# One transformer block in split fp32 on one core: w_out as a Strassen product, its weights and the first gate_up weights split during the projections, sums and low halves on GpSimd

## The chip, the cores and the metric

The kernel runs on one core of a Trainium2 chip. The metric is device microseconds for one execution of the whole block. A core has five engines, each with its own instruction queue that runs in order: TensorE (PE in the profile, its weight loads PEld) for matmuls, VectorE (DVE), ScalarE (ACT) and GpSimd (POOL) for elementwise work, and SyncE (SP), which issues most DMA transfers; GpSimd issues some as well. They wait for each other on semaphores.

## The reference, cut to what matters

```python
D_MODEL = SEQ = 1024; ATTN_WIDTH = CONV_WIDTH_CH = 512; FFN_HIDDEN = 2816; DEPTH = 1

def mixer(h, w_in, b_f, conv_w, w_branch, w_out):
    proj = jnp.einsum("bsd,dn->bsn", h, w_in)
    q, k, v, f_logit, g_b, g_c, hc, gate_conv, gate_attn = jnp.split(proj, _SPLITS, axis=-1)
    ya = g_b * causal_depthwise_conv(g_c * hc, conv_w)
    ...
    yb = forgetting_attention(q.reshape(shp), k.reshape(shp), v.reshape(shp), logf)
    ya_d = jnp.einsum("bsc,cd->bsd", ya, w_branch[0])
    yb_d = jnp.einsum("bsc,cd->bsd", yb, w_branch[1])
    merged = jax.nn.sigmoid(gate_conv) * ya_d + jax.nn.sigmoid(gate_attn) * yb_d
    return jnp.einsum("bsd,de->bse", merged, w_out)

def swiglu(h, w_gate_up, w_down):
    gu = jnp.einsum("bsd,df->bsf", h, w_gate_up)
    g, u = jnp.split(gu, 2, axis=-1)
    return jnp.einsum("bsf,fd->bsd", jax.nn.silu(g) * u, w_down)

    # reference, per layer
    h = rmsnorm(x, norm_mix_pre[l])
    m = mixer(h, w_in[l], b_f[l], conv_w[l], w_branch[l], w_out[l])
    x = x + rmsnorm(m, norm_mix_post[l])
    h = rmsnorm(x, norm_ffn_pre[l])
    f = swiglu(h, w_gate_up[l], w_down[l])
    x = x + rmsnorm(f, norm_ffn_post[l])
```

All tensors are float32, with 1024 rows of 1024.

## The kernel before

**Split products.** Each float32 operand is kept as two float32r tiles, a high half (ScalarE copies and rounds) and a low half (VectorE subtracts the high half from the original). `split` makes both; `mm3` issues three matmuls per 128x128 weight block: high by high, low by high, high by low.

**Strassen.** In the projections, gate_up and down, a product is done on 2x2 blocks with seven block products in the Winograd form: A11, A12, A22 of the left operand, its sums S1 to S4, and B11, B21, B22 and the sums T1 to T4 of the right operand. A block product (`prod`) is 4 blocks x 3 = 12 matmuls of 128x512, and a job of seven is 84. `strassen` issues them in the order S2, S1, S3, S4, A22 in two PSUM banks, b2 and b3: VectorE must have taken b2 into a sum before S3 adds to it, and b3 before S4 does. The product A11 (`first`, b1) is copied out by ScalarE before A12 adds to the same bank.

**Stages, in order.** The projections: 18 jobs, to about 400 us. Attention with the branch products `pba`, to 567 us. The second branch product `pbb`: 16 tiles (2 column halves `n` x 8 blocks `d` of 128), each with a load of the saved gate `sg` and then, on VectorE, gate times product and an addition into `um`, the merged rows, held transposed (feature blocks by 1024 rows). During its first half `w_out` is loaded in 8 pieces and split into `woh` and `wol`. Then w_out itself: `e_mm(st)` splits 128 rows of `um` and multiplies by all of w_out, 2 halves x 8 blocks x 3 matmuls (`pm`); `e_norm(st)` norms, adds x, norms again, and 8 transposes (`tp`) put the rows back into `um`. Then the f stage: `f_first(f)` for seven of the gate_up jobs loads the job's first weights from `w_gate_up`, splits them, and makes A11 and A12, which go to `pre_dram` until the job needs them; `h2_sums(sl)` makes T1 to T4 and B22 of the right operand of gate_up between them. Then gate_up (771 to 1126 us) and down (to 1343 us).

**Order.** Every call goes through `InOrder.call` at line 76, so that nearly all rows of the profile have that line; they are told apart by the names of their tiles. The Tile framework orders each engine's instructions by its own estimates; calls within a `strict` stretch keep the order of the code on the engines named. Tiles are reused in rings (`raw`, `hi`, `lo`, `sx`): a load or a write waits until the last reader of the tile's former contents is done.

## Time and profile before

| | |
|---|---|
| median of three runs | 1350.23 us (1350.2 to 1351.78) |
| the profiled execution's own time | 1350.04 us |
| its span in the profile | 1348.2 us |
| PE busy | 1328.5 us, 6753 matmuls |
| DVE, ACT, POOL busy | 932.3, 535.2, 127.2 us |
| granted PE clock | 0.999 |

Busy times are sums over the span; each engine's idle time matters only where PE waits for that engine. In the views a row names engine, operation, output tile, input tiles and shape; "<-" behind a bracketed time names what ended the idle time. The share of DMA is of the core's 16 DMA engines.

### The profile page before, as it was taken

Reading aid. Unit: us, or ns where it says so; the run is one execution under the profiler, and the core shown is the slowest. Engines: PE = TensorE matmul, PEld = TensorE weight load, DVE = VectorE, ACT = ScalarE, POOL = GpSimd, SP = SyncE. Lnnn points to the kernel's source line nnn. Section 1 sums busy time; section 2 is a strip of 40 time slices with the busy share of each in tenths; the row PEclk is TensorE's granted clock in tenths of the full one; section 3 lists DMA queues with packets and bytes.
Section 4 is the critical chain, followed back from the end, with each engine's and each line's share of the span. In section 5 each row is a group of like instructions: output and inputs, shape, how many; then the busy total and the mean of one; then the engine's idle time right before and its main releaser. Section 6 shows DMA issues by size and latency. Waiting matters only on the chain.

```text
span 1348.2 us, 17709 instructions
## 1 busy us (share of the span) xinstructions
PE 1328.5 (99%) x6753; PEld 1098.9 (82%) x6753; DVE 932.3 (69%) x1445; ACT 535.2 (40%) x851; POOL 127.2 (9%) x252
## 2 busy tenths in 40 slices
PE   9999999999999999999999999999999999999997
PEld 7978888888887778788887788888888888888886
DVE  6974668754556766775669698776677766677585
ACT  6642222243345756613547232223222323444452
POOL 0001000011112112000002121100111011000000
PEclk9999999999999999999999999999999999999999
DMA  5332422333325444362235565332323236965541
GB/s 189 118 109 86 126 70 71 105 123 109 102 82 192 158 142 165 126 218 79 94 110 175 170 200 167 102 100 80 117 102 118 93 111 240 361 235 196 161 164 63
DMA packets 153256, 186.36 MB, mean 138 GB/s; under 512 B 9409, under 2 KB 106753, under 8 KB 153170
## 3 DMA queue, kind: packets, MB, share of 16 engines
q1 hardware_dynamic: 138434, 136.67, 32.4%
q0 software_dynamic: 14736, 48.54, 9.3%
q8 instruction: 53, 0.87, 0.3%
q14 instruction: 33, 0.27, 0.1%
HBM read 136.10 MB, written 49.09 MB: 137 GB/s over the span
## 4 chain that ended last, share of the span: by engine, by line
PE 58%; DVE 3%; DMA 2%; issue 1%; ACT 1%; POOL 0%; DVEq 0%; SPq 0%; POOLq 0%; ACTq 0%
PE b L76 28%; PE pd L76 15%; PE pm L76 5%; PE pbb L76 3%; PE pba L76 2%; PE po L76 1%; PE tps L76 1%; PE sp L76 1%; DMA pre_dram<-s 1%; DMA tk<-in_w_down_dram 1%; DVE tt L76 0%; DVE lo L76 0%; PE tp L76 0%; DMA pre_dram<-c 0%; ACT tt L76 0%
## 5 line engine op out<-in xcount | busy, mean ns | idle before, releaser
L76 DVE TENSOR_TENSOR c<-c,b 128x512 f32<-128x512 f32 x195 | 132.9, 682 | 91.4 <-PE b L76 72.3
L76 DVE TENSOR_TENSOR lo<-raw,hi 128x1024 fp32r<-128x1024 f32 (+1 forms) x93 | 112.0, 1204 | 83.1 <-PE b L76 68.8
L76 ACT ACTIVATE hi<-raw 128x1024 fp32r<-128x1024 f32 (+1 forms) x100 | 101.7, 1018 | 127.9 <-PE b L76 75.7
L76 PE MATMUL b<-hth,hi 128*128 128x512 f32 x352 | 137.3, 390 | 0.0
L76 PE MATMUL b<-hth,lo 128*128 128x512 f32 x352 | 137.0, 389 | 0.0
L76 PE MATMUL b<-htl,hi 128*128 128x512 f32 x352 | 136.9, 389 | 0.0
L76 ACT ACTIVATE hi<-sx 128x1024 fp32r<-128x1024 f32 x41 | 43.5, 1062 | 220.9 <-PE b L76 195.3
L76 PEld LDWEIGHTS b<-hth,hi 128*128 128x128 f32 x352 | 66.1, 188 | 14.6 <-DVE c L76 1.0
L76 PEld LDWEIGHTS b<-hth,lo 128*128 128x128 f32 x352 | 66.1, 188 | 13.8
L76 PEld LDWEIGHTS b<-htl,hi 128*128 128x128 f32 x352 | 66.1, 188 | 13.7
L76 DVE TENSOR_TENSOR lo<-sx,hi 128x1024 fp32r<-128x1024 f32 x41 | 50.2, 1224 | 33.6 <-PE b L76 31.4
L76 PE MATMUL b<-hah,hi 128*128 128x512 f32 x176 | 69.0, 394 | 1.2 <-ACT c L76 1.2
L76 PE MATMUL b<-hal,hi 128*128 128x512 f32 x176 | 68.5, 389 | 0.0
L76 PE MATMUL b<-hah,lo 128*128 128x512 f32 x176 | 68.4, 390 | 0.0
L76 DVE TENSOR_TENSOR sx<-raw 128x512 f32<-128x512 f32 x78 | 53.6, 688 | 19.1 <-DMA raw<-in_w_in_dram 9.0
L76 PE MATMUL pd<-hi,lo 128*128 128x512 f32 x160 | 62.3, 389 | 0.0
L76 PE MATMUL pd<-hi 128*128 128x512 f32 x160 | 62.0, 390 | 0.0
L76 PE MATMUL pd<-ghi 128*128 128x512 f32 x148 | 57.6, 390 | 0.0
L76 PE MATMUL pd<-glo,ghi 128*128 128x512 f32 x148 | 57.6, 389 | 0.0
L76 PE MATMUL pd<-ghi,glo 128*128 128x512 f32 x148 | 57.6, 389 | 0.0
L76 PE MATMUL b<-hT34h,hi 128*128 128x512 f32 x136 | 53.0, 390 | 0.4 <-DVE c L76 0.4
L76 PE MATMUL b<-hT34h,lo 128*128 128x512 f32 x136 | 52.9, 389 | 0.0
(368 smaller groups left out, 3359.9 us busy)
## 6 DMA issues: line engine op xcount, KB each, us to landing
raw<-in_w_gate_up_dram SPq DMA_DIRECT2D x51, 512.0 KB, 3.8
raw<-in_w_in_dram SPq DMA_DIRECT2D x35, 512.0 KB, 3.8
a_dramS<-um POOLq DMA_DIRECT2D x44, 256.0 KB, 2.8
a_dramA<-um POOLq DMA_DIRECT2D x33, 256.0 KB, 2.8
xt<-in_x_dram SPq DMA_DIRECT2D x16, 512.0 KB, 4.3
sg<-sg_dram SPq DMA_DIRECT2D x32, 256.0 KB, 4.6
graw<-a_dramS SPq DMA_DIRECT2D x14, 512.0 KB, 4.0
sg_dram<-c POOLq DMA_DIRECT2D x24, 256.0 KB, 2.3
```

Source lines behind the costliest of these rows:

```text
L76: ins = getattr(self.engine, name)(*args, **kw)
```

## The change

**w_out as a Strassen product.** Its rows are taken in four pairs of 128-row tiles: of a pair, a11 and a12 are the two feature halves of the first tile, a21 and a22 of the second. Seven block products of 12 matmuls stand for each pair. `first(i)` and `second(i)` make A11 and A12 of all pairs ahead, `strassen` the other five products pair by pair.

**The combined weights.** B11, B21, B22 and T1 to T4 of w_out are made in the projections: `wo_load(n)`, one in each of the jobs 1 to 16, loads four 128x128 pieces, makes four differences on GpSimd, splits seven pieces (128x896) at the job's end and stores high and low halves to `wo_dram` at the start of the next. The `pbb` stage loads them back, a piece of 512 KB beside each `sg`.

**The first gate_up weights.** `pw_load(f)`, in the jobs 1 to 7, loads 512 KB, splits 128x1024 and stores two halves to `pw_dram`; `f_first` loads these instead of splitting.

**GpSimd.** It makes the sums S1 to S4 of the rows in `um` (16 of 128x512, `sums_31` and `sums_24`), the low halves of S2, S3, S1 with A22, and S4 (`gsplit`), 11 of the multiplications by the gain `gpo`, two of four subtractions of `h2_sums`, and the low half of `hc`.

```diff
@@ projections, per job
+    def wo_load(n):
+        k, c = divmod(n, 4)
+        r, h, l = w0_tiles()
+        for slot, (row, half) in enumerate(((k, 1), (k, 0), (4 + k, 0), (4 + k, 1))):
+            c0 = half * NC + c * P
+            nc.sync.dma_start(r[:, slot], wout_d[row * P : (row + 1) * P, c0 : c0 + P])
+        for o, a, b in ((4, 0, 1), (5, 3, 4), (6, 3, 0), (7, 2, 5)):
+            gtt(r[:, o], r[:, a], r[:, b], ALU.subtract)
...
     for ij, (kind, j, _, _) in enumerate(jobs):
+        for _, store in side.pop(ij - 1, ()):
+            pinned(store, "sync")
+        if 0 < ij < len(jobs) - 1:
+            side[ij] = [wo_load(ij - 1)] + ([pw_load(ij - 1)] if ij <= NPRE else [])
...
+        for ops, _ in side.get(ij, ()):
+            pinned(lambda: split(*ops), "vector", "scalar")
@@ pbb
             nc.sync.dma_start(sg, sg_dram[d][1, :, ns])
+            load_wo(*loads.pop(0))
...
-            if n == 0:
-                wr = flat(raw_t())
-                nc.sync.dma_start(wr, wout_d[d * P : (d + 1) * P, :])
-                split(woh[:, d, :], wol[:, d, :], wr)
+            if n and d == 1:
+                first_ops(0, [s4h_t(), s4h_t()], [s4l_t(), s4l_t()])
+                sx = wtile("sx", 1)
+                for i in range(2):
+                    sums_31(i, sx[:, 4 * i : 4 * i + 4])
+                sums_24(0)
@@ w_out
+    def sums_31(i, t):
+        a11, a12, a21, a22 = blocks(i)
+        s3[i] = t
+        gtt(t, a11, a21, ALU.subtract)
+        gtt(a21, a21, a22, ALU.add)
+    def sums_24(i):
+        a11, a12, s1, a22 = blocks(i)
+        gtt(a11, s1, a11, ALU.subtract)
+        gtt(a12, a12, a11, ALU.subtract)
...
+    def rest_ops(i):
+        a = slice(2 * i * P, (2 * i + 1) * P)
+        b = slice((2 * i + 1) * P, (2 * i + 2) * P)
+        hx, lx = hi_t(), lo_t()
+        gsplit(hx[:, LO], lx[:, LO], um[:, LO, a])
+        h1, l1 = hi_t(), lo_t()
+        gsplit(h1, l1, um[:, :, b])
+        gsplit(hx[:, UP], lx[:, UP], s3[i])
+        h4, l4 = s4h_t(), s4l_t()
+        gsplit(h4, l4, um[:, UP, a])
...
+    def e_norm(i, c12, c21, c22):
+        qa, qb = qas[i], st2("qb")
+        for c, acc in ((c12, qb[:, 0:1]), (c21, qa[:, 1:2]), (c22, qb[:, 1:2])):
+            square(c, acc)
+        for c, ns in ((c12, n2), (c22, n2)):
+            gtt(c, c, gpo[:, ns], ALU.mult)
+        if i < PAIRS - 1:
+            gtt(c21, c21, gpo[:, n1], ALU.mult)
...
+                nc.vector.scalar_tensor_tensor(
+                    xt[:, ns], c, rs[:, e : e + 1], xt[:, ns], op0=ALU.mult, op1=ALU.add
+                )
...
+    for step in (0, 1, 2, 3):
+        first(step)
+        if step:
+            second(step - 1)
+    second(PAIRS - 1)
...
     def f_first(f):
-        w, _ = prep_first(f_src(f)[0])
-        b1, p1 = strassen_first(w, hb, psm, fp)
+        h1, l1 = hi_t(), lo_t()
+        for t, d in zip((h1, l1), pw_dram[f]):
+            nc.sync.dma_start(f32(flat(t)), d)
+        b1 = bank(psm, "b1")
+        prod(b1, (h1[:, LO], l1[:, LO]), hb[B11], True)
...
+        copy(p1, b1)
+        prod(b1, (h1[:, UP], l1[:, UP]), hb[B21], False)
...
+    ops = rest_ops(0)
+    for i in range(PAIRS):
+        nxt = rest_ops(i + 1) if i + 1 < PAIRS else None
+        _, *cur = strassen(
+            ops, wob, psm, fe, keeps[i][:, 0], (lambda: e_turn(i - 2)) if i > 1 else None
+        )
+        e_norm(i, *cur)
+        if i > 1:
+            half_split(B11, i - 2)
+        ops = nxt
...
+    f_first(0, p1_of(0), lambda: e_turn(2))
+    h2_sums(0)
+    f_first(1, p1_of(1))
+    h2_sums(1)
+    f_first(2, p1_of(2))
+    f_first(3, p1_of(3), lambda: e_turn(3))
...
+    for sl in range(2, 4):
+        h2_sums(sl)
...
+    for f in range(4, NPRE):
+        f_first(f)
```

GpSimd's queue from the end of attention on, with the change. Ahead of it stand attention's multiplications by `mask`, as before; `um` is the merged rows, `sx` and `s4_6050` hold S3 of pairs 0, 1 and 2, `s4l` and `lo` are low halves, `raw_6081` is c21 of pair 0.

```order
L76 TENSOR_TENSOR sx_5895<-um_3800 128x512 x2
L76 TENSOR_TENSOR um_3800<-um_3800 128x4x128 x4
L76 TENSOR_TENSOR s4_6050<-um_3800 128x512
L76 TENSOR_TENSOR um_3800<-um_3800 128x4x128 x3
L76 TENSOR_TENSOR s3_6059<-um_3800 128x512
L76 TENSOR_TENSOR um_3800<-um_3800 128x4x128 x5
L76 TENSOR_TENSOR s4l_6205<-um_3800,s4h_6204 128x512
L76 TENSOR_TENSOR s4l_6219<-um_3800,s4h_6218 128x512
L76 TENSOR_TENSOR lo_6195<-um_3800,hi_6194 128x512
L76 TENSOR_TENSOR lo_6195<-sx_5895,hi_6194 128x512
L76 TENSOR_TENSOR lo_6199<-um_3800,hi_6198 128x1024
```

Before, GpSimd had DMA issues alone from here to the end. The 16 sums come first (six of them while `pbb` still runs), and the last row is the low half of S1 and A22 of pair 0.

VectorE's queue in w_out with the change, from the x updates of pair 0 on. `c12`, `raw_6081` and `c22` were multiplied by `gpo` on GpSimd; `b3_6357` is the bank of pair 1's S1, which S4 adds to next.

```order
L76 SCALAR_TENSOR_TENSOR xt_6034<-raw_6081,r1_6309,xt_6034 128x512
L76 SCALAR_TENSOR_TENSOR xt_6034<-c12_6236,r1_6309,xt_6034 128x512
L76 SCALAR_TENSOR_TENSOR xt_6036<-raw_6081,r1_6309,xt_6036 128x512
L76 SCALAR_TENSOR_TENSOR xt_6036<-c22_6250,r1_6309,xt_6036 128x512
L76 TENSOR_TENSOR c22_6384<-raw_6096,b3_6357 128x512
L76 TENSOR_TENSOR c22_6384<-c22_6384,b2_6356 128x512
```

The sums that empty the banks of one pair stand behind the x updates of the pair before; pairs 1 and 2, and 2 and 3, follow one another in the same way.

SP's queue in the projections: before, all of the weight loads of the jobs (`raw`, 512 KB each), which stood among few others.

```order
L76 DMA raw<-in_w_in_dram 128x8x128 x12
L76 DMA cb<-c_dram 128x1024 x2
L76 DMA raw<-in_w_in_dram 128x8x128 x10
L76 DMA kl<-qk_dram_67 128x1024
L76 DMA raw<-in_w_in_dram 128x8x128 x2
```

With the change, the stretch with the stores of one job's side work, the side loads of the next job and that job's first store:

```order
L76 DMA raw<-in_w_in_dram 128x8x128
L76 DMA wo_dram<-l_1808 128x7x128
L76 DMA pw_dram_128<-hg 128x1024
L76 DMA pw_dram_128<-lg 128x1024
L76 DMA r_1954<-in_w_out_dram 128x128 x4
L76 DMA rg<-in_w_gate_up_dram 128x8x128
L76 DMA raw<-in_w_in_dram 128x8x128
L76 DMA wo_dram<-h_1955 128x7x128
L76 DMA raw<-in_w_in_dram 128x8x128 x2
```

One or two loads of `raw` now stand between stores that wait for splits.

276 lines of the change are left out of this document (180 added, 96 removed).

## The prediction

> **What bounds the kernel now.** I read the page first, to see which engine is full.
>
> ```profile
> span 1348.2 us, 17709 instructions
> PE 1328.5 (99%) x6753; PEld 1098.9 (82%) x6753; DVE 932.3 (69%) x1445; ACT 535.2 (40%) x851; POOL 127.2 (9%) x252
> PEclk9999999999999999999999999999999999999999
> ```
>
> PE is busy for 99% of the span at an undisturbed clock, so time goes where matmuls go, and a stage gains only if nothing makes PE wait in their place. Next comes the chain of waits around w_out (start, length, what). `pbb` is the branch product ahead of w_out, `pm` w_out itself, `tp` the transposes after it, and the first `b` row the seven split-ahead gate_up products that I call the f stage.
>
> ```profile
> 567.59 43.52 PE pbb L76 x192
> 611.11 21.55 PE pm L76 x95
> ...
> 644.94 1.09 PE tp L76 x8
> ...
> 705.57 18.47 PE b L76 x78
> 724.06 1.22 DVE lo L76
> 725.28 1.21 DVE tt L76
> ...
> 738.43 4.49 DMA pre_dram<-s
> 745.55 4.80 DMA pre_dram<-c
> ...
> 759.69 3.78 DMA raw<-in_w_gate_up_dram
> ...
> 769.69 1.21 DVE lo L76
> 771.64 354.18 PE b L76 x1560
> ```
>
> The long PE rows give the pitch of a matmul: 354.18/1560 = 0.227 us, and 43.52/192 is the same. The chain leaves PE only between 724 and 772, in the f stage and the start of gate_up. How much PE loses there is in the busy time by stretch (columns: stretch, length, then PE, PEld, DVE, ACT and POOL busy, clock, DMA share, GB/s).
>
> ```profile
> 567.00:611.00 44.00, 44.00 (x196) 36.44 (x195) 34.02 (x46) 13.62 (x17) 0.00 (x0) 1.00 0.57 179
> 611.00:706.00 95.00, 94.65 (x444) 77.99 (x443) 59.66 (x129) 40.77 (x89) 3.77 (x7) 1.00 0.29 100
> 720.00:775.00 55.00, 51.68 (x225) 40.54 (x224) 42.38 (x62) 25.39 (x37) 9.57 (x18) 1.00 0.55 177
> ```
>
> w_out has no gap worth naming (0.35 us of 95). From 720 to 775 PE stands 55 - 51.68 = 3.3 us. That is all the idle time that the change can take away; the rest of its gain must be matmuls.
>
> **Removed: matmuls.** w_out falls from 8 row tiles x 2 halves x 8 blocks x 3 = 384 matmuls to 4 pairs x 7 products x 12 = 336. 48 x 0.227 = 10.9 us. Transposes stay 64. Against the profiled execution, 1350.04 us (1.8 above its span, and 0.2 below the median of the three runs): 1339.1.
>
> **Removed: waits in the f stage.** The first gate_up weights no longer are split there; they come in finished. Which of the 3.3 us goes? The waits of PE (total, times, longest) name the releasers, and the timeline shows one of them.
>
> ```profile
> PE b L76 <- DVE c L76: 2.5, 3, 1.5
> PE b L76 <- ACT c L76: 2.1, 3, 1.2
> ```
>
> ```profile
> 726.54 0.50 PE L76 MATMUL b<-hah,hi 128*128 128x512 f32 x1 [1.16 <-ACT c L76]
> ```
>
> The 1.16 us at 726.54 is PE waiting for ScalarE's copy of the first product out of PSUM before the second adds to it. The new f_first has the same copy in the same place, so I keep that wait and take 3.3 - 1.2 = 2.1 us as gone (bounds 0 and 3.3).
>
> **Added: GpSimd in front of every left operand.** Call the end of `pbb` 611.1. PE then does eight products whose operands VectorE and ScalarE make (8 x 12 x 0.227 = 21.8 us, until 632.9), and only then S2, S1, S3, S4, A22 of pair 0, 2.7 us each. These need GpSimd: ten sums on `um` after the last `um` addition, low halves of 512 for S4 of pairs 0 and 1 and for S2 and S3 of pair 0, and one of 1024 for S1. GpSimd's one arithmetic row and the rows of VectorE for such work are these, by form (count, busy us, mean ns, idle time before); below them, from the timeline, the rhythm of `pbb`'s end:
>
> ```profile
> L76 POOL TENSOR_TENSOR cb<-cb,mask 128x128 f32<-128x128 f32 x64 | 28.9, 460 | 103.4 <-DVE nm L76 98.4 <-DMA cb<-c_dram 4.4
> L1602 POOL MEMSET const-float32-0.0<- 128x1 f32 x1 | 0.1, 98 | 0.2 <-issue 0.2
> L76 DVE TENSOR_TENSOR um<-um 128x512 f32<-128x512 f32 x44 | 30.1, 684 | 0.3
> L76 DVE TENSOR_TENSOR lo<-um,hi 128x1024 fp32r<-128x1024 f32 x8 | 9.7, 1222 | 8.4 <-PE pm L76 8.0
> L76 DVE SCALAR_TENSOR_TENSOR um<-um,r,x2t 128x512 f32<-128x512 f32 x16 | 11.1, 747 | 0.2
> L76 DVE SCALAR_TENSOR_TENSOR tt<-xt,r,gpr 128x1024 f32<-128x1024 f32 x8 | 10.3, 1284 | 0.2
> ```
>
> ```profile
> 608.43 0.69 DVE L76 TENSOR_TENSOR sg<-sg,pbb 128x512 f32<-128x512 f32 x1 [1.31 <-PE pbb L76]
> 609.15 0.69 DVE L76 TENSOR_TENSOR um<-um,sg 128x512 f32<-128x512 f32 x1
> ```
>
> No 128x512 GpSimd operation is in this trace. Let p be its price. Lower bound: VectorE's 0.68. Upper: four of the 460 ns, 1.84. Nearest is GpSimd's own row with the fixed 98 ns of a near-empty instruction taken out: 0.098 + 4 x 0.362 = 1.55, and 3.0 for 1024. I take 1.55.
>
> The Trainium skill's "GPSIMD Engine Reference" (section 3.1) measured 4497 ns for an fp32 addition of 2048 elements per partition; a line through that and the 460 ns here would make p about 1.27, an estimate. With it the lateness worked out next would be nil and the sum 1.5 us lower; no row of 512 elements here tests it.
>
> The last `um` addition ends as the rows at 608.43 and 609.15 say, two VectorE operations after the last matmul: 612.5. Then 10 sums + 4 halves at p + one at 2p - 0.1 = 16p - 0.1 us of GpSimd. p = 1.55: 637.2. S1's low half is wanted at 632.9 + 2.7 + 0.2 = 635.8. **Late by 1.5 us.** At 1.84 it is 6.0 late, at 0.68 early.
>
> The next place is pair 1. VectorE's queue holds its x updates, which wait for GpSimd's multiplications by gpo, ahead of the sum that empties the bank for pair 2's S4; PE waits for that bank. Until the last of pair 1's multiplications GpSimd has 28 operations of p, three of 2p - 0.1 and two DMA issues of about 0.54: 34p + 0.8. PE wants the bank at 632.9 + 27.2 (two pairs) + 8.2 + 2.2 (16 transposes by the 1.09) = 670.5, less VectorE's 0.75 + 0.69: 669.0. GpSimd is there at 612.5 + 34p + 0.8: 666.0 at 1.55, in time; 675.9 at 1.84, 6.9 late (not on top of the 6.0, since a late start is already in it). So the GpSimd term is **+1.5**, bounds 0 and 7.
>
> **Moved: h2 sums and the start of gate_up.** The last transposes end at 632.9 + 54.4 + 4.4 + three f products pairs and a half (19.0) + 4.4 = 715.1. VectorE then has four subtractions and eight low halves of 512 (12 x 0.68 = 8.2, to 723.3). The raw tile that they free takes a 3.8 us load (the chain's row at 759.69), then three sums, ScalarE's 1.06, VectorE's 1.22: about 731.5. PE wants it at 715.1 + 19.0 = 734.1. Covered by 2.6 us, by the f4 to f6 products; if GpSimd's two subtractions in the chain cost 1.84 each, by 2.0. I put +0.5 for it, bounds 0 and 3 (the stall of before, moved).
>
> **Added to the projections.** Per job (84 matmuls, 19.05 us): VectorE 1.1 and, in seven jobs, 1.2 more; ScalarE the same less a little; four GpSimd operations of 0.46; five to nine DMA issues on SP, two to four of them stores that wait for splits.
>
> ```profile
> 148.00:262.00 114.00, 114.00 (x505) 94.38 (x505) 80.91 (x116) 26.33 (x31) 4.37 (x8) 1.00 0.31 90
> 262.00:396.00 134.00, 134.00 (x593) 110.97 (x592) 73.51 (x98) 49.49 (x66) 16.56 (x31) 1.00 0.34 108
> ```
>
> ```profile
> raw<-in_w_in_dram SPq DMA_DIRECT2D x35, 512.0 KB, 3.8
> ```
>
> (The rows above: the first eight jobs or so, the rest, and the landing time of a 512 KB weight load.) VectorE goes from 71% (80.91/114) to 83% in the seven jobs; DMA share from 0.31 by 2.7 MB in 19 us (142 GB/s at the row's 0.0034 per GB/s) to 0.8. PE's cover is whole jobs of its own work, since weights are made one job ahead. A raw load that stands on SP behind a waiting store is what could be late: the split ends, the load takes 3.8, and then come the sums. I put +0.5 in all, bounds 0 and 16 (1 us in each of 16 jobs). In `pbb` the loads rise from 8.4 to 12.6 MB (16 of 256 KB as before, and 16 instead of 8 of 512 KB): share 0.57 x 1.5 = 0.86. Tight, but under one: 0.
>
> **Sum.** 1350.04 - 10.9 - 2.1 + 1.5 + 0.5 + 0.5 = **1339.5 us**.
>
> **Rivals.** *Clean*: GpSimd is at p below 1.45, all 3.3 us go, nothing is late: 1339.1 - 3.3 = 1335.8. For it: slack of 2 to 3 us at every later place. *GpSimd slow*: p = 1.84, 7 late instead of 1.5: 1345. Against it: a fixed part surely exists. *GpSimd and VectorE take turns*: where both read two operands from SBUF, one may stand while the other works. In this trace GpSimd's 64 multiplications hardly overlap such VectorE work (in attention it reads scores from PSUM), so their 460 ns say nothing of it. Per pair VectorE has 4 x 0.75 + 2 x 1.28 + 1.22 = 6.8 us of such work and GpSimd 8p + 1 = 13.4; in turns 20.2 against PE's 13.6 to 15.8. If GpSimd alone gives way, it loses 8.0 us by the bank of pair 2 (two low halves of 1.22 ahead of the first pairs and pair 0's six x updates, 5.6): 666.0 + 8.0 - 669.0 = 5 late, 1343. If VectorE's seven operations also wait a whole p each, VectorE has 3.4 (five sums) + 6.8 + some 2 of small ones + 10.9 = 23 per pair, 7 us lost in each of three: 1359. It is **slower than before** once VectorE waits over about 1.2 us per operation on three pairs (some 15 us in all). *Queue*: SP's stores hold back raw loads in the projections: 1 us in the seven jobs is 1346, in all 16 it is 1355.
>
> The rule for taking turns stands in the Trainium skill, "SBUF — State Buffer", section "Who interferes with whom": a VectorE instruction with two SBUF inputs and a GpSimd instruction that reads SBUF exclude each other for the whole instruction. By that rule the result would lie in that rival's 1343 to 1359; no row of this trace shows it.
>
> **How the numbers follow.** Forecast (1337 to 1343) 0.48; clean 0.15; GpSimd slow 0.12; turns 0.15; queue 0.10. A measurement here can tell 0.2% (2.7 us) from no change: faster is below 1347.5, slower above 1352.9. Faster: 0.48 + 0.15 + 0.12 + 0.04 of turns + 0.04 of queue = 0.83; same 0.05 + 0.03; slower 0.06 + 0.03. The range 1335 to 1349 leaves out the lower half of clean and the upper halves of turns and queue.
>
> **What would show it.** PE with 48 fewer 128x512 matmuls of the same pitch; GpSimd's 128x512 rows at 1.3 to 1.8 us, S1's first matmuls of pair 0 waiting for `lo` from POOL by 1 to 2 us, and hardly a POOL wait elsewhere; the wait for ScalarE's copy still in the f stage; no new waits from 68 to 400. VectorE rows of two SBUF inputs longer than 0.75 and 1.28 in this stage would show the turns. A PE wait for raw loads' sums in the projections would make the prediction wrong in its smallest term.

## The result: 1368.16 us, slower by 1.3%, and the profile after

The changed kernel takes 1368.16 us (median of 4 runs, 1366.81 to 1368.47) beside 1350.26 us for the kernel before on the same chip: a ratio of 1.0128, with a 95% interval of 1.011 to 1.0145. Forecast were 1339.5 us and a range of 1335 to 1349. The page of the profiled execution (span, busy time of each engine with its instructions):

```profile
span 1366.1 us, 18114 instructions
PE 1326.0 (97%) x6705; PEld 1094.2 (80%) x6705; DVE 957.8 (70%) x1423; ACT 549.8 (40%) x872; POOL 251.2 (18%) x371
```

The matmuls are 48 fewer, as counted, and yet the span is 17.9 us longer. The chain of waits after the change (start, length, what), from the second branch product on:

```profile
579.64 43.52 PE pbb L76 x192
623.16 35.15 PE b L76 x155
658.39 0.90 ACT hi L76
...
661.43 1.22 DVE va L76
```

Two things are to be seen. `pbb` starts at 579.6 instead of 567.6, so 12 us are lost ahead of it. And in the w_out stage, where the chain used to run on PE without a break, it now leaves PE 35 us after `pbb` and runs on VectorE, through the norms. The busy time by stretch (columns as in the prediction) gives the sizes:

```profile
68.00:148.00 80.00, 75.60 (x319) 61.54 (x320) 46.27 (x71) 26.97 (x34) 15.53 (x28) 0.96 0.58 176
148.00:262.00 114.00, 109.81 (x474) 89.24 (x473) 89.41 (x122) 35.91 (x42) 18.26 (x28) 0.99 0.72 205
262.00:410.00 148.00, 148.00 (x655) 122.55 (x654) 91.20 (x118) 59.27 (x77) 35.52 (x65) 1.00 0.60 170
...
579.00:623.00 44.00, 44.00 (x196) 36.43 (x195) 29.18 (x40) 5.79 (x9) 10.60 (x7) 1.00 0.78 275
623.00:720.00 97.00, 89.00 (x411) 72.59 (x410) 64.68 (x103) 46.68 (x93) 59.62 (x44) 1.00 0.53 187
720.00:800.00 80.00, 71.27 (x306) 56.62 (x305) 63.19 (x82) 36.03 (x58) 32.93 (x39) 0.96 0.62 203
```

The sum of the 17.9 us: +12.05 up to the start of `pbb` (579.5 against 567.4 by its first matmul); +4.85 from there to the first matmul of down (568.5 us instead of 563.7, although 10.9 us of matmuls are gone); +0.95 behind it. In w_out PE stands 97 - 89.0 = 8.0 us where it stood 0.35, and from 720 to 800 8.7 us where it stood 3.3 (720 to 775 before). The clock column is 0.96 in two of the stretches with waits.

**The projections.** The first new wait is at their start. Two gate_up loads of the side work (`rg`) go out on SP at 67.84 and 68.88 us, just ahead of v's last store, which GpSimd issues at 69.02. ScalarE's copy of the first product waits for that store to land; before, it waited for PE alone (ScalarE's timeline, the change first):

```profile
74.16 0.60 ACT L76 ACTIVATE c<-b 128x512 f32<-128x512 f32 x1 [5.55 <-DMA v_dram<-vs]
...
71.96 0.60 ACT L76 ACTIVATE c<-b 128x512 f32<-128x512 f32 x1 [3.13 <-PE b L76]
```

PE stands 3.11 us for that copy instead of 0.69, and its next 13 matmuls start 0.43 us apart instead of 0.227: some 5.2 of the 12.05 us. The rest, some 6 us, is lost at three job ends, at 149, 210 and 226. At 210 PE waits 1.78 us for the sum `c<-c,b` at 209.54. The timeline of all engines ahead of it:

```profile
199.02 2.15 SPq L76 DMA_DIRECT2D r<-in_w_out_dram  x4
...
203.21 2.27 POOL L76 TENSOR_TENSOR r<-r 128x128 f32<-128x128 f32 x3 [0.42 <-DMA r<-in_w_out_dram]
...
205.51 0.95 ACT L76 ACTIVATE h<-r 128x896 fp32r<-128x896 f32 x1 [5.08 <-POOL r L76]
...
207.32 1.04 ACT L76 ACTIVATE hi<-sx 128x1024 fp32r<-128x1024 f32 x1
...
208.39 1.23 DVE L76 TENSOR_TENSOR lo<-sx,hi 128x1024 fp32r<-128x1024 f32 x1 [3.47 <-ACT hi L76]
209.54 0.68 DVE L76 TENSOR_TENSOR c<-c,b 128x512 f32<-128x512 f32 x1
210.27 0.50 PE L76 MATMUL b<-hT34h,hi 128*128 128x512 f32 x1 [1.78 <-DVE c L76]
```

`r` are the w_out pieces, `h` their high halves; `hi<-sx` and `lo<-sx` are the next job's own weights. The pieces were loaded at 199, GpSimd subtracts until 205.5, and ScalarE, whose next instruction is the split of these pieces, stands 5.08 us for it. Behind it in ScalarE's queue are the split of the gate_up piece and the next job's; VectorE stands 3.47 us for that, and behind VectorE's low half is the sum that empties the bank that PE wants.

**w_out.** VectorE and GpSimd at the first wait (timeline of all engines, their rows):

```profile
661.34 1.28 POOL L76 TENSOR_TENSOR raw<-raw,gpo 128x512 f32<-128x512 f32 x1
661.43 1.22 DVE L76 TENSOR_SCALAR va<-qa 128x2 f32<-128x2 f32 x1
...
668.24 2.41 POOL L76 TENSOR_TENSOR lo<-um,hi 128x1024 fp32r<-128x1024 f32 x1
668.57 2.12 DVE L76 TENSOR_SCALAR va<-ssq 128x2 f32<-128x2 f32 x1
...
672.05 2.34 POOL L76 TENSOR_TENSOR s4l<-um,s4h 128x512 fp32r<-128x512 f32 x1 [1.39 <-ACT s4h L76]
673.16 2.32 DVE L76 SCALAR_TENSOR_TENSOR raw<-xt,r,gpr 128x1024 f32<-128x1024 f32 x1
```

A VectorE operation on two columns, mostly 0.16 us in this stage, ends when GpSimd's operation ends: 661.43 + 1.22 is 661.34 + 1.28 plus 0.03, and 668.57 + 2.12 is 668.24 + 2.41 plus 0.04. It also goes the other way: GpSimd's `s4l` takes 2.34 us instead of the 1.29 that it takes at 656.32, where VectorE is idle or reads PSUM. From 623 to 721 the chain of waits holds no row of GpSimd itself: its results were not what came late. Ten VectorE operations on two columns took 0.5 to 2.4 us there, 12.3 in all, which is 10.7 more than at 0.16 each.

**The start of gate_up** (the same view, ScalarE and PE):

```profile
749.24 0.63 ACT L76 ACTIVATE x<-raw 128x512 fp32r<-128x512 f32 x1 [1.09 <-POOL raw L76]
...
751.34 1.06 ACT L76 ACTIVATE c<-b 128x512 f32<-128x512 f32 x2
...
751.97 1.22 PE L76 MATMUL b<-x,hi 128*128 128x512 f32 x2 [4.68 <-ACT c L76]
```

PE waits 4.68 us for ScalarE's copy of a first product (of f4; before, the longest wait for such a copy in the f stage was 1.16, of f3), because ahead of it on ScalarE stand the high halves of h2's sums, which wait for GpSimd's subtractions. The wait of 3.22 us at 727, for f1's copy, has the same picture. Behind the 4.68 the matmuls start 0.43 us apart instead of 0.227 (the first two 0.6), for about ten matmuls: the clock column is 0.55 from 752 to 757 us.

### The profile page after: what moved, and what is told of

Same layout as the page of the kernel before. It is cut to its first block, busy times and chain, and to the rows that moved or that the text cites. A ratio compares the mean times of both kernels' runs of the same rounds, so it can differ in the third digit from the quotient of the medians.

```text
span 1366.1 us, 18114 instructions
## 1 busy us (share of the span) xinstructions
PE 1326.0 (97%) x6705; PEld 1094.2 (80%) x6705; DVE 957.8 (70%) x1423; ACT 549.8 (40%) x872; POOL 251.2 (18%) x371
## 4 chain that ended last, share of the span: by engine, by line
PE 53%; DVE 6%; issue 1%; DMA 1%; ACT 1%; POOL 1%; DVEq 0%; SPq 0%; ACTq 0%; POOLq 0%
PE b L76 29%; PE pd L76 15%; PE pbb L76 3%; PE pba L76 2%; PE po L76 1%; PE tps L76 1%; PE sp L76 1%; DVE x L76 1%; DVE raw L76 1%; DVE c L76 1%; DVE va L76 1%; DVE xt L76 1%; ACT junk L76 1%; DMA tk<-in_w_down_dram 1%; DVE tt L76 0%
## 5 line engine op out<-in xcount | busy, mean ns | idle before, releaser
L76 PE MATMUL b<-x,hi 128*128 128x512 f32 x1232 | 382.4, 392 | 10.8 <-ACT c L76 4.7
L76 PEld LDWEIGHTS b<-x,hi 128*128 128x128 f32 x1232 | 231.3, 189 | 61.8 <-ACT sx L76 5.6
L76 PE MATMUL b<-x,lo 128*128 128x512 f32 x616 | 240.4, 390 | 0.0
L76 DVE TENSOR_TENSOR lo<-raw,hi 128x1024 fp32r<-128x1024 f32 x86 | 104.6, 1216 | 73.4 <-PE b L76 57.9
L76 PEld LDWEIGHTS b<-x,lo 128*128 128x128 f32 x616 | 116.1, 188 | 24.5
L76 ACT ACTIVATE hi<-sx 128x1024 fp32r<-128x1024 f32 (+1 forms) x43 | 44.7, 1040 | 181.2 <-PE b L76 158.0
L76 POOL TENSOR_TENSOR r<-r 128x128 f32<-128x128 f32 x64 | 39.8, 642 | 131.1 <-DMA r<-in_w_out_dram 130.0
L76 PE MATMUL b<-hT34l,hi 128*128 128x512 f32 x136 | 53.4, 393 | 0.0
L76 PE MATMUL b<-hT12h,hi 128*128 128x512 f32 x136 | 52.9, 389 | 0.0
L76 PE MATMUL b<-hT12h,lo 128*128 128x512 f32 x136 | 52.9, 389 | 0.0
```

Of the source, the lines that this page charges most:

```text
L76: ins = getattr(self.engine, name)(*args, **kw)
```

## The experiments

Three theories stood at first. **Turns**: GpSimd's work beside VectorE's stretches both. **Side work**: the projections' extra splits, stores and loads delay the next weights, by their amount or by their place. **Matmuls**: something in the seven-product form itself is slow. All runs of the block in one table (totals are medians, ratio to the kernel before on the same chip with its interval; then, of the profiled run, the first `pbb` matmul and the time from there to the first matmul of down, in us). The profiled run is within 2.1 us of the median but for three kernels, where it was the slowest of its runs, 3.4 to 7.1 above the median: `side_gp_store` (1398.66), `all_vector` (1359.61) and `vector_no_side` (1345.01).

| kernel | total | ratio | `pbb` at | `pbb` to down |
|---|---|---|---|---|
| before | 1350.2 | 1 | 567.4 | 563.7 |
| after | 1368.16 | 1.0128 [1.011, 1.0145] | 579.5 | 568.5 |
| side_alone | 1360.51 | 1.0073 [1.0058, 1.0088] | 578.6 | 564.0 |
| no_side | 1359.71 | 1.0068 [1.0051, 1.0085] | 567.5 | 572.2 |
| all_vector | 1354.96 | 1.0035 [1.0023, 1.0046] | 579.9 | 558.8 |
| h2_vector | 1364.71 | 1.0104 [1.0089, 1.0119] | 579.0 | 567.2 |
| vector_no_side | 1341.59 | 0.9943 [0.9931, 0.9955] | 567.1 | 555.2 |
| side_pw_late | 1357.68 | 1.0049 [1.0033, 1.0066] | 575.9 | 564.4 |
| side_wo_alone | 1356.55 | 1.0053 [1.0039, 1.0066] | 572.5 | 563.9 |
| side_gp_store | 1391.61 | 1.0319 [1.0294, 1.0343] | 615.4 | 563.9 |
| side_after_prep | 1360.74 | 1.0075 [1.0061, 1.0088] | 579.0 | 563.9 |
| side_end_step | 1361.49 | 1.0083 [1.0069, 1.0096] | 576.5 | 563.6 |
| side_spaced | 1366.83 | 1.0117 [1.0103, 1.0132] | 583.6 | 564.1 |
| best1 | 1384.43 | 1.0257 [1.0238, 1.0277] | 603.6 | 559.0 |
| best2 | 1355.30 | 1.0041 [1.0028, 1.0053] | 576.0 | 558.0 |
| best3 | 1353.97 | 1.0027 [1.0016, 1.0037] | 577.9 | 555.5 |
| best4 | 1352.72 | 1.0015 [1.0006, 1.0024] | 579.0 | 555.6 |
| best5 | 1356.63 | 1.0053 [1.004, 1.0066] | 583.4 | 553.9 |
| best6 | 1351.72 | 1.0012 [1.0003, 1.0021] | 577.5 | 553.9 |

### The two engines by themselves

`turns` computes nothing of the block: it copies x out and runs GpSimd and VectorE on tiles of their own, first alone, then together, and then lets PE wait for chains of VectorE sums of growing length.

> Not the block: a small kernel that copies x to the output and then times operations of the two engines by themselves and together, in parts that both begin together; last, PE runs 180 matmuls and waits for a growing chain of VectorE sums, nine lengths, each twice. In the changed kernel's trace a GpSimd operation of 512 took 1.29 us where VectorE was still and up to 2.3 beside it, and VectorE's 128x2 tensor_scalar took 0.15 or 1.2 to 2.4. Theory 'turns': GpSimd alone 1.27 to 1.3 (512) and 2.4 (1024); beside VectorE operations with two SBUF inputs (sum, or x update) one waits for the other, so that the two sums of times add: 16 x 1.29 + 24 x 0.68 = 37 us for the part in place of 21; beside operations that read PSUM and SBUF both as alone, 21 us; beside 128x2 operations VectorE's rows up to 1.3 us. Rival 'bandwidth or measuring': all parts 21 us, rows longer but overlapping. PE: if the clock falls after one wait of about 3.4 us, pitches of 0.43 after the waits of five sums (3.4 us and what the copy takes) and longer, none after two or three; if it falls by the busy share of some window, shorter waits show it in some of the two tries.

Operations by form, in the stretch in which the engines run one after the other:

```profile
L72 DVE TENSOR_TENSOR vo<-va,vb 128x512 f32<-128x512 f32 x12 | 8.3, 692 | 0.5
...
L72 DVE TENSOR_SCALAR vt<-vs 128x2 f32<-128x2 f32 x24 | 4.1, 170 | 0.8
L72 POOL TENSOR_TENSOR go<-ga,gb 128x512 f32<-128x512 f32 x12 | 15.2, 1264 | 0.9
```

And together, pair by pair in three later stretches (16 of GpSimd beside 24 sums of two SBUF tiles, beside 24 sums with one PSUM input, beside 60 operations on two columns):

```profile
L72 DVE TENSOR_TENSOR vo<-va,vb 128x512 f32<-128x512 f32 x24 | 31.7, 1319 | 1.0 <-POOL va L72 0.2
L72 POOL TENSOR_TENSOR go<-ga,gb 128x512 f32<-128x512 f32 x16 | 25.5, 1596 | 1.2
...
L72 DVE TENSOR_TENSOR vo<-va,bank 128x512 f32<-128x512 f32 x24 | 16.5, 688 | 0.9
L72 POOL TENSOR_TENSOR go<-ga,gb 128x512 f32<-128x512 f32 x16 | 20.3, 1266 | 1.2
...
L72 DVE TENSOR_SCALAR vt<-vs 128x2 f32<-128x2 f32 x60 | 25.3, 422 | 2.3 <-POOL vs L72 0.3
L72 POOL TENSOR_TENSOR go<-ga,gb 128x512 f32<-128x512 f32 x16 | 20.3, 1268 | 1.2
```

Sums from SBUF go from 0.69 to 1.32 us, GpSimd's from 1.26 to 1.60: both lose, VectorE more. VectorE's part takes 32.5 us, nearer to the 37 of strict turns than to the 21 of the rival: a pair comes every 1.67 us, where the two add to 1.96, so some of each pair still overlaps. The x updates lose as much (0.75 to 1.34 us). A PSUM input takes VectorE out of it altogether (0.688, and 1.266 for GpSimd). The operations on two columns go from 0.17 to 0.42 on average (one that starts inside a GpSimd operation takes about 1.1 and ends with it); GpSimd loses nothing to these. So the turns are real here, and one 128x512 GpSimd operation alone is 1.26, not the 1.55 of the forecast.

From here on a wait of PE is counted from the start of one matmul to the start of the next; the idle time in a row's bracket is 0.39 us less, which is how long a matmul takes, and without a wait the starts are 0.227 apart. After waits of 1.6 us (2 tries) no matmul was slow; after waits of 2.36 to 8.2 us (16 tries), 6 to 14 matmuls started about 0.43 us apart each time, some 1.4 to 3.0 us on top of the wait, with a clock column of 0.50 there (450.87 to 456 us). Two sums were enough for it, not the five of the first expectation.

### Which half of the change loses what

`side_alone` is the kernel before with the projections' side work only (nobody reads its results). `no_side` is the change without that work; the weights are read from one stored tile, so its output is not the block's.

```diff
--- side_alone: before, plus wo_load, pw_load, their splits and stores
--- no_side: after, with
-        if 0 < ij < len(jobs) - 1:
+        if False:
             side[ij] = [wo_load(ij - 1)] + ([pw_load(ij - 1)] if ij <= NPRE else [])
```

> The kernel before with the side work of the projections alone: w_out's combined weights and the first gate_up weights are loaded, split and stored as in the change, and then not used; w_out and the f stage are those of before. Theory 'projections': the 12.0 us by which the changed kernel reaches the second branch product late are the side work's and of nothing else: 1350.2 + 12.0 = 1362.2 (1361 to 1364), with the same waits at 71, 208 and 224 us. Rival 'layout': the tiles' places and what follows share in it: under 1357.

> The changed kernel without the side work of the projections: no combined weights and no gate_up weights are made there; the later loads read one 512 KB tile of split weights in their place, so that the output is not the block's. Theory 'projections': 1368.2 - 12.0 = 1356.2 (1355 to 1358), w_out and the f stage still 5.8 us behind the kernel before. Rival 'late weights': the loss behind the branch products comes partly from the stores' or loads' lateness: under 1354.

Alone, the side work costs 10.3 us (1360.51 against 1350.2; 0.5 under the range expected), all of it before `pbb` (578.6). Without it the projections end at 567.5 as before, and still the rest of the change loses 8.5 us behind them (572.2 - 563.7), and 9.5 in total, 1.7 above the range expected. The two halves lose in different places, each makes the kernel slower by itself, and their sum, 19.8, is near the 17.9 of both together.

`all_vector` moves all of GpSimd's arithmetic behind the branch products to VectorE; `h2_vector` only those of `h2_sums` and `hc`.

```diff
--- all_vector (vtt: tensor_tensor on VectorE; gsplit_ = split; h2_vector: the last two places alone)
-        gtt(t, a11, a21, ALU.subtract)
+        vtt(t, a11, a21, ALU.subtract)
...
-        gtt(w[:, LO], b22, b12, ALU.subtract)
+        vtt(w[:, LO], b22, b12, ALU.subtract)
...
-        gsplit(hch[:, :, a], hcl[:, :, a], um[:, UP, b])
+        gsplit_(hch[:, :, a], hcl[:, :, a], um[:, UP, b])
```

> The changed kernel with all of GpSimd's arithmetic behind the branch products on VectorE (sums, low halves, multiplications, h2 sums). Theory 'turns': the loss of 16.7 us of waits behind the branch products is mostly VectorE and GpSimd standing for each other: 1368.2 less 4 to 8 = 1360 to 1364 although VectorE gets 27 us more in w_out. Theory 'VectorE's queue': the x updates and their norm stand ahead of the sums that empty the banks, however the rest is shared out: with 27 us more work on that queue 1373 to 1385.

> The changed kernel with the subtractions of h2_sums and the low half of hc on VectorE again; w_out's sums, low halves and multiplications stay on GpSimd. Theory 'chain of both': the waits of 3.6 and 5.1 us in the f stage, with the slow matmuls behind, come from GpSimd and VectorE working by turns on one chain that ScalarE's queue waits for: 1368.2 less 5 to 8 = 1360 to 1363. Theory 'sigmoid': ScalarE stands at gate_up's first sigmoid, and the waits stay: 1366 to 1368.

`all_vector` is 13.2 us faster than the change by the medians, 5.0 below the range expected, and 9.7 from `pbb` to down in the profiled runs. Its w_out stage by stretch:

```profile
623.00:720.00 97.00, 96.30 (x445) 78.99 (x444) 79.40 (x154) 52.32 (x105) 5.95 (x11) 1.00 0.59 214
720.00:790.00 70.00, 62.92 (x269) 50.10 (x269) 50.43 (x76) 29.47 (x47) 12.46 (x23) 0.95 0.61 191
```

VectorE does all the work, 79.4 us in 97, and PE stands 0.7 us; with GpSimd's help VectorE was busy for 64.7 and PE stood 8.0. None of its 50 operations on two columns takes over 0.3 us. The turns are the w_out loss. What is left of waits from 720 on is not GpSimd's arithmetic: the longest, 4.8 us, ends with ScalarE, which stands 4.11 us in front of gate_up's first sigmoid (at the load of its table) for a read-back from `pre_dram`, ahead of copies that PE wants:

```profile
730.24 1.28 ACT L76 ACT_TABLE_LOAD   x1 [4.11 <-DMA c<-pre_dram]
```

`h2_vector` takes back 3.5 us by itself, between the ranges of its two theories (1.4 from `pbb` to down in the profiled runs).

`vector_no_side` is both at once, with that sigmoid and the first two read-backs kept in their written places (output not the block's, as in `no_side`).

> The change without its side work (the combined weights and gate_up's first weights are read from one stored tile instead, so the output is not the block's), with GpSimd's arithmetic behind the branch products on VectorE and the start of gate_up pinned. If side work and GpSimd's turns with VectorE are the two causes and add up, branch products begin at 567.5 and the down projection 555 to 558 us later: 1350.2 - 6 to -8.5 = 1341.5 to 1344.5. If something else in the change costs time too (reading the seven weight sets, the extra sums on VectorE), it is above 1346.

1341.59 us: 8.6 us faster than before, 26.6 faster than the change, and 2.1 from the forecast. So nothing is wrong with the seven-product form, and these causes (side work, turns, the order at the start of gate_up) are the whole miss. That it comes near the forecast does not confirm the forecast's sum: VectorE does here what the forecast gave to GpSimd, and the side work is gone.

### Why the side work costs time: its amount or its place

`side_wo_alone` has the w_out pieces only; `side_pw_late` moves the gate_up pieces two jobs on (jobs 3 to 9); `side_gp_store` lets GpSimd issue the stores, so that SP's raw loads stand behind none.

```diff
--- side_wo_alone, from side_alone
-            side[ij] = [wo_load(ij - 1)] + ([pw_load(ij - 1)] if ij <= NPRE else [])
+            side[ij] = [wo_load(ij - 1)]
--- side_pw_late, from side_alone (and the loads of rg pinned)
+            side[ij] = [wo_load(ij - 1)] + ([pw_load(ij - 1 - 2)] if 0 <= ij - 1 - 2 < NPRE else [])
--- side_gp_store, from side_alone
-            pinned(store, "sync")        # nc.sync.dma_start(wo_dram ..., pw_dram ...)
+            pinned(store, "gpsimd")      # nc.gpsimd.dma_start(...)
```

> The kernel before with one half of the side work alone, the combined weights of w_out in 16 jobs, without the gate_up pieces. Theory 'gate_up pieces': they bring the early wait and the last microsecond of lateness in the jobs 6 to 8, and the w_out pieces alone cost 0 to 2 us: 1350 to 1352. Rival 'w_out pieces': 1354 to 1357, with waits at 188 to 225 us.

> The kernel before with the side work alone, as in side_alone, but the seven gate_up pieces in the jobs 3 to 9 instead of 1 to 7, and their loads kept behind the earlier loads of SP. Theory 'first loads': two of those loads, issued at 68 us, delay the store of v that ScalarE's copy waits for; this one wait of 3.8 us and the slow matmuls behind it are some 5 of the 10.1 us of side_alone: 1360.5 - 5 = 1355.5 (1354.5 to 1357). Rival 'amount': the same amount of DMA delays something wherever it stands: 1359 or more.

> The kernel before with the side work alone, as in side_alone, but its stores are issued by GpSimd instead of SP, so that no load of SP stands behind a store that waits for a split. Theory 'SP's queue': the waits of PE at 188 and 225 us (2.7 and 1.8 us, and slow matmuls behind the first) go, the one at 72 us stays: 1360.5 - 5 = 1355.5 (1354.5 to 1357). Rival 'splits': ScalarE's and VectorE's added 2 us each per job, ahead of the splits that PE needs, are the cause: 1359 to 1361.

The w_out pieces alone lose 5.0 us by the start of `pbb` (6.5 by the medians), in waits at the ends of jobs (0.53, 1.06, 0.86, 1.09 and 2.04 us). Moving the gate_up pieces gives 2.8 us of the 5 expected; it takes away the first wait, at 71 us, that two of their loads had caused at the start, but other waits come in later jobs (at 204, 220, 275 and 284 us). The stores on GpSimd failed badly: 31 us more. They now stand in one queue with the `qk` and `sg` stores and GpSimd's own subtractions, and one wait alone is 11.4 us: before it, ScalarE stands 13.09 us for four subtractions, which GpSimd begins at 155.60, right behind two such stores. What held the first of these (issued at 154.47, long after its split) the profile does not show. The waits of `side_wo_alone` that were followed back (at 184 and 204) have the picture shown above of the change; here the one at 184 (timeline of all engines):

```profile
180.94 0.95 ACT L76 ACTIVATE h<-r 128x896 fp32r<-128x896 f32 x1 [5.81 <-POOL r L76]
181.80 1.04 ACT L76 ACTIVATE hi<-sx 128x1024 fp32r<-128x1024 f32 x1
...
182.88 1.22 DVE L76 TENSOR_TENSOR lo<-sx,hi 128x1024 fp32r<-128x1024 f32 x1 [0.88 <-ACT hi L76]
184.02 0.68 DVE L76 TENSOR_TENSOR c<-c,b 128x512 f32<-128x512 f32 x1
...
184.76 0.50 PE L76 MATMUL b<-hT34h,hi 128*128 128x512 f32 x1 [0.48 <-DVE c L76]
```

And the same weights in the kernel before (the same view):

```profile
177.90 1.06 ACT L76 ACTIVATE hi<-sx 128x1024 fp32r<-128x1024 f32 x1 [7.40 <-PE b L76]
...
180.86 1.23 DVE L76 TENSOR_TENSOR lo<-sx,hi 128x1024 fp32r<-128x1024 f32 x1 [1.56 <-PE b L76]
```

This is what "one job ahead" is worth: the split of the next weights waits for PE itself (by the code, to free a tile of the ring), and so it comes late in the job. With the pieces it starts 3.9 us later (181.80 against 177.90), about one of them from earlier waits, and PE waits 0.86 (0.48 idle): a ScalarE that stands for GpSimd at that moment has some 2 us to give, an estimate from these numbers, not a job.

Three more places for the same work. `side_after_prep` puts the step of each job behind the preparation of the next weights; `side_end_step` puts it at the job's end, with each split meant to be a whole job behind its loads; `side_spaced` is the first again, but jobs 2, 3 and 16 load no piece and jobs 10, 12 and 14 load two. In all three the gate_up pieces are in the jobs from 8 or 9 on, and attention's first `cb` loads move to job 16.

```diff
--- side_after_prep
+            w = pairs.get()
+            side_step(ij)          # split and store piece n, then load piece n + 1
-            c11, c12, c21, c22 = strassen(pairs.get(), h1b, psm, pp)
+            c11, c12, c21, c22 = strassen(w, h1b, psm, pp)
--- side_end_step: the same three calls behind the job's outputs, from job 0 on
--- side_spaced
+            side_step(ij, ij not in (2, 3, 16))
+        if ij in (10, 12, 14):
+            side_step(0)
+            side[0] = [wo_load(pieces.popleft())]
```

> The kernel before with the whole side work of the projections (w_out's weights and gate_up's, gate_up's in jobs 9 to 15), nothing else of the change, and with its step moved: in each job ScalarE's and VectorE's split of the raw columns stands behind the preparation of the next job's own weights and ahead of the job's products, a whole job after the loads and GpSimd's four subtractions; its stores stand behind it, then the next loads. Theory 'a split that waits for GpSimd stands ahead of the next weights' split on ScalarE and VectorE': the waits at the job ends of the run with w_out's pieces alone (0.53 + 1.06 + 0.86 + 1.09 + 2.04 us, branch products beginning 5.1 us late) go, since the result that the split needs is then 20 us old; branch products begin within 1.5 us of 567.4, total 1350 to 1352. Rival 'the work itself (about 1.2 us of ScalarE, 1.0 us of VectorE, 2.8 us of GpSimd in each job of 20 us) or its transfers are the loss, wherever it stands': branch products begin at 572 or later as before, total 1355 or more.

> The kernel before with all of the side work and nothing else of the change; its step now stands once at the end of each job from the first: the split of the columns loaded a whole job (about 20 us) before, its stores, then the next loads. Theory 'place': the two waits of 4.7 us (at 164) and 4.4 us (at 407) and the waits at the job ends are both gone, branch products begin by 569, total 1350 to 1352. Rival 'the work itself or its transfers': branch products at 572 or later, total 1355 or more.

> The kernel before with all of the side work and nothing else of the change; its step stands behind the preparation of the next weights, as in the run that had only the waits at 164 us (4.7) and 407 us (4.4), but jobs 2, 3 and 16 load no piece of w_out (three later jobs take a second piece instead), so that no split stands directly behind its own loads. Theory 'distance between loads and split': both waits go and none comes in their place but where a job has two pieces (up to 1 us each); branch products begin by 570, total 1350 to 1353. Rival 'the work costs it wherever it stands': branch products at 574 or later, total 1356 or more.

By their totals all three missed (1360.74, 1361.49 and 1366.83 us); by the places of their waits they answer the question. In `side_after_prep` the waits at the job ends are gone, as ScalarE shows in the job of the rows above:

```profile
175.55 0.95 ACT L76 ACTIVATE h<-r 128x896 fp32r<-128x896 f32 x1 [0.72 <-POOL r L76]
...
184.13 1.06 ACT L76 ACTIVATE hi<-sx 128x1024 fp32r<-128x1024 f32 x1 [7.14 <-PE b L76]
...
406.39 0.95 ACT L76 ACTIVATE h<-r 128x896 fp32r<-128x896 f32 x1 [5.80 <-POOL r L76]
```

`hi<-sx` waits for PE again, as before the change. But two new waits of 4.7 and 4.4 us stand at 164 and 407, where two steps come so close together that the split stands behind its own loads (the last row). In `side_end_step` the split at 181.41 still follows its loads, issued at 173.14, by only 8 us, and the job-end waits are back. In `side_spaced` PE loses nothing until 297 us, and then 8.12, 2.87 and 3.14 us, in the three jobs with two pieces. The work moved; the waits followed the short distances.

### Versions that mend both

All have GpSimd's arithmetic on VectorE as in `all_vector`. `best1`: stores on GpSimd and gate_up pieces late. `best2`: pieces in jobs 9 to 15, the first sigmoid and read-backs pinned. `best3`, `best4` and `best5` have the places of `side_after_prep`, `side_end_step` and `side_spaced`. `best6` has one piece per job and no split straight behind its loads: the first piece is split at the end of job 1, job 3 has no step, and the sixteenth piece, for which no job is left, is split in the attention.

```diff
--- best2 to best6, the start of gate_up
-            nc.scalar.activation(sg, g, AF.Sigmoid)
+            pinned(lambda: nc.scalar.activation(sg, g, AF.Sigmoid), "scalar")   # f == 0
+            pinned(lambda: nc.gpsimd.dma_start(t, d), "gpsimd")                 # read-backs, f < 2
--- best6, the side work
+        if ij not in (0, 3, len(jobs) - 1):
+            side_split()
+            side_load(ij)
...
+        if ij == 1:
+            side_split()
+            side_load(ij)
+        if ij == len(jobs) - 1:
+            side_split()
```

> All of w_out's and the f stage's arithmetic on VectorE and ScalarE (all_vector), the seven gate_up pieces in the jobs 3 to 9, stores of the side work issued by GpSimd, and gate_up's first sigmoid kept behind the copies of the f stage on ScalarE. If both theories on the projections hold, 10 to 12 us go there; if the 4.8 us wait of all_vector at 730 us is ScalarE standing at that sigmoid for the read-back of its operand, 4 to 6 more: 1355.0 - 15 = 1340 (1338 to 1344). If only the turns of GpSimd and VectorE mattered: 1353 to 1356.

> All of w_out's and the f stage's arithmetic on VectorE and ScalarE (all_vector); the seven gate_up pieces in the jobs 9 to 15, where the changed kernel has no wait of PE, with attention's first loads behind them; stores on SP again; gate_up's first sigmoid on ScalarE, and three of the read-backs for its first two jobs on GpSimd's queue, kept behind the f stage's copies and stores. If GpSimd's turns, the place of the gate_up pieces and those queue orders are the causes: all_vector's 1355.0 less some 8 in the projections and some 6 in the f stage, 1341 (1338 to 1346). If the w_out pieces alone cost the projections most: 1348 to 1352.

> The change with the three repairs together: GpSimd's arithmetic behind the branch products on VectorE; the side work's step behind the preparation of the next job's weights, with gate_up's pieces in jobs 9 to 15; in gate_up the first sigmoid and the first two columns' read-backs in their written places. Theory 'all of the loss lies in where the new work stands': the projections end 0 to 1.5 us late instead of 12.05, and from the branch products' start to the down projection the time is 557 to 558 us (563.7 before: the run without GpSimd's arithmetic had 558.8, its successor 557.9, each with one wait of 3.7 to 4.8 us that halved the clock behind it; without that wait 553 to 555); total 1350.2 + 1 - (6 to 10) = 1341 to 1345, faster than both. Rival 'the transfers of the side work cost what they cost': branch products 5 us late or more, total 1348 to 1351.

> The change with both repairs: GpSimd's arithmetic behind the branch products on VectorE, the start of gate_up pinned, and the side work's step once at each job's end behind loads a job old. Theory: branch products by 569 as in the run of this step alone, and 555 to 558 us from there to the down projection (its predecessor had 555.4): total 1350.2 + 1.5 - 5.7 to -8.3 = 1343.4 to 1346, faster than the kernel before. Rival: the waits move on and it stays at 1350 or above.

> The change with GpSimd's arithmetic behind the branch products on VectorE, the start of gate_up pinned, and the side work's step as in the run before it. Theory: branch products by 570, 555 to 556 us from there to the down projection (its two predecessors had 555.4 and 555.6), total 1350.2 + 2.5 - 8.2 = 1343 to 1346, faster than the kernel before. Rival: branch products at 574 or later and a total of 1348 or more.

> The change with GpSimd's arithmetic behind the branch products on VectorE, the start of gate_up pinned, and one step of the side work per job behind the next weights' preparation, none with a split straight behind its own loads: the first piece is split at the end of job 1, job 3 has no step, and the last piece is split in the attention behind the last job. In the run before it jobs 0 to 9 lost nothing, and only the three jobs with a second piece waited (8.12, 2.87 and 3.14 us). Theory 'distance between loads and split': branch products by 569.5, then 555 to 556 us to the down projection, total 1350.2 + 2 - 8.2 = 1342.5 to 1345.5, faster than the kernel before and within 3 us of the change without side work and without GpSimd's turns (1341.59). Rival 'the work costs it wherever it stands': branch products at 573 or later, total 1348 or more.

`best1` carries the cost of the GpSimd stores. From `pbb` to down all are 4.7 to 9.8 us faster than before. In `best2` one 3.70 us wait was left there, for f6's store behind a read-back on GpSimd's queue; pinning that too took it away (555.5 in `best3`). All six were expected at 1338 to 1346, and all missed: the totals of `best2` to `best6` stay 1.6 to 6.5 us above the kernel before, for what is lost ahead of `pbb`. `best6` shows that part by stretch:

```profile
148.00:262.00 114.00, 114.00 (x505) 94.37 (x504) 86.59 (x120) 33.62 (x39) 20.12 (x36) 1.00 0.62 157
262.00:397.00 135.00, 135.00 (x597) 111.61 (x596) 91.65 (x115) 61.92 (x79) 27.10 (x54) 1.00 0.80 245
397.00:440.00 43.00, 37.12 (x239) 29.18 (x237) 20.26 (x33) 17.88 (x29) 11.39 (x20) 0.92 0.66 212
```

From 148 to 397 us PE does not stand at all, with 13 of the 16 pieces and all seven of gate_up, at a DMA share of 0.80 and VectorE at 68% (91.65/135). The work and its transfers cost nothing there. The first matmul of the last job comes at 397.3 us instead of 395.5, late by one wait at 94 us. Then 5.9 us and a clock of 0.92 are lost at one place, the sixteenth piece (timeline of all engines):

```profile
424.01 0.94 ACT L76 ACTIVATE h<-r 128x896 fp32r<-128x896 f32 x1
...
424.98 0.37 SPq L76 DMA_DIRECT2D wo_dram<-h  x1
...
426.64 0.56 SPq L76 DMA_DIRECT2D lo<-qk_dram  x1
...
433.98 0.63 ACT L76 ACTIVATE hi<-lo 128x512 fp32r<-128x512 f32 x1 [5.91 <-DMA lo<-qk_dram]
```

Its stores wait on SP for the split, and attention's load of q (`lo<-qk_dram`, issued at 411.76 in the kernel before) stands behind it and is some 13 us later; ScalarE stands 5.91 us for it, and PE is idle 5.1 us for ScalarE. This is a relative of the rival that the forecast called queue: a store that waits for a split holds back a load, here attention's and not a raw one. `best6` is at 1.0012 of the kernel before, no gain, and no version that was run and has the block's output is faster than the kernel before. Without that one wait it would be about 1343 (1351.72 less the 8.3 us by which `pbb` falls back between 397 and 577), an estimate; that was not run.

## Why the prediction was wrong, step by step

Two steps made the miss: the side work of the projections, put at +0.5 and measured at 12.05, and GpSimd beside VectorE from w_out on, whose turns the sum left at nothing. The gain in matmuls was as forecast.

**Removed matmuls, -10.9: right.** 48 fewer, at the same pitch; and `best5` and `best6` are both 9.8 us faster from `pbb` to down.

**Waits in the f stage, -2.1: wrong.** PE stands 8.7 us there instead of 3.3. The step that failed is "The new f_first has the same copy in the same place, so I keep that wait": such copies now have ScalarE's high halves of GpSimd's sums ahead of them, and where one wait of 1.16 stood there are two, of 3.22 and 4.68 (idle time).

**GpSimd in front of every left operand, +1.5: its price was too high, its neighbour's was left out.** p is 1.26 alone, near the estimate of 1.27 worked out from "GPSIMD Engine Reference", section 3.1, of the Trainium skill, not 1.55. S1 of pair 0 was in time, as that estimate had it (the lateness itself is 637.2 - 635.8 = 1.4 by the prediction's numbers, not 1.5). But "GpSimd is there at ... 666.0 at 1.55, in time" priced the bank by when GpSimd is done; the chain holds no GpSimd row there, and it was VectorE's own operations ahead of the bank's sum that ran longer beside it (on two columns, 0.16 to as much as 2.37). w_out lost 8.0 us of PE time there, and 0.7 once GpSimd was out of it.

**Turns, given 0.15: what happened from w_out on.** It cost 13.2 us by the medians (1368.16 against 1354.96), 9.7 between `pbb` and down in the profiled runs. The rule of the Trainium skill, "SBUF — State Buffer", section "Who interferes with whom", held in its direction: beside GpSimd, VectorE loses with two SBUF inputs and not with a PSUM input. Shut out for the whole instruction, as the prediction put it, they were not quite: a pair took 1.67 us, not 1.96. The rival's working had the mechanism but the wrong victim: it counted the large operations only (6.8 us a pair). The operations on two columns, half a dozen to a norm and each at the mercy of a GpSimd operation of 1.3 or 2.4 us, lie in the chain from ScalarE's squares to the bank's sum, and "some 2 of small ones" priced them at nothing extra: ten of them took 10.7 us more.

**h2 sums and the start of gate_up, +0.5: too small.** Moving only these off GpSimd gave 3.5 us by the medians, just outside the bound of 3 (1.4 from `pbb` to down in the profiled runs).

**Projections, +0.5: the largest miss, 12.05.** It is within the bounds of 0 to 16, but the value was chosen by "PE's cover is whole jobs of its own work, since weights are made one job ahead". The cover was some 2 us, since the next split begins only when PE lets it. Nor was "a raw load that stands on SP behind a waiting store" the main path, though a like one came up in `best6`: at the job ends the split itself stood on ScalarE for GpSimd, ahead of the next weights' split. And some 5.2 of the 12.05 were lost before any job end, where the side loads held up v's store; the sum had priced the loads by their share of the DMA alone.

**`pbb` loads, 0: right.** PE 44.00 of 44, at a share of 0.78.

**The rivals were weighed one against the other**, as if one excluded the next. Turns and the projections' waits are in different stages, and they add up. And no term stood for the clock: in the change 2.8, 1.6 and 2.2 us of slow matmuls, behind the waits at 74.8, 226 and 752 us.

## What to carry to other kernels

Before work is put on an idle GpSimd, look at what VectorE does in the same microseconds: where it reads SBUF (two tiles, or a few columns in a chain), GpSimd's help can cost more than it takes over; beside sums with a PSUM input it was free (0.688 and 1.266, as alone). A step added to an in-order queue is not priced by its length but by how long it may stand and what is queued behind it, and the slack of that is read from what the instruction behind waited for before: one that waits for PE, for a ring tile, is made just in time, however far ahead its loads run. Side work wants its operands a whole step old, by the clock and not by the line of code; with that, jobs carried it at a DMA share of up to 0.80 for nothing.

## What the runs showed of the hardware that was not expected

VectorE operations on 128x2, with a scalar and one input, also wait for GpSimd: 0.17 alone and 0.42 on average beside it, up to 2.1 to 2.4 in the w_out stage, while GpSimd lost nothing to them (1.268). A wait of PE of 2.36 us was enough to be followed by 6 to 14 matmuls at about half the rate, in all 16 tries from there on in `turns`; in the block's kernels a longer one was not always followed by it (the wait of 3.61 us at 727 in the changed kernel was not, the same wait, 3.62 us, in `no_side` was, for 13 matmuls), and what decides between them stays open.
